# Attention's order in a piece, the joint latent norms, a last row pair by 7 products, and which row pairs of the heads and of the query latent go by 7

## The chip, the cores and the metric

The kernel runs on one core of one Trainium2 chip. The metric is the device time of one execution in microseconds, as the median of several runs; lower is better. The engines are named as in the profile: PE is TensorE's matmul, PEld its weight load, DVE VectorE, ACT ScalarE, POOL GpSimd, SP SyncE. SP issues the loads of the weights; GpSimd's queue carries the DMAs that read and write the stream x.

## The reference

A decoder trunk of two layers over 256 tokens of 2048 features in float32: retention with an MLP, then latent attention (MLA) with an MLP. What matters here:

```python
x = x + retention(rms_norm(x), w_in, w_out)      # 8 heads: q, k 256 wide, v, gate 512 wide
x = x + sq_relu_mlp(rms_norm(x), w1, w2)         # 2048 -> 8192 -> 2048, relu squared

down = rms_norm(x) @ w_kv_down                   # 512 latent columns, 64 of the rotary key
c_kv = rms_norm(down[..., :512])
k_pe = apply_rope(rms_norm(down[..., 512:]))
k_nope, v = split(c_kv @ w_kv_up)                # 16 heads of 128 and 128
c_q = rms_norm(rms_norm(x) @ w_dq)               # the query latent, 1536 wide
q_nope, q_pe = split(c_q @ w_uq)                 # each normed per head, q_pe rotated
p = softmax(causal(scale * (q_nope @ k_nope.T + q_pe @ k_pe.T)))
x = x + (p @ v) @ w_o
x = x + sq_relu_mlp(rms_norm(x), w1, w2)
```

## The kernel before

**Products in three matmuls.** Each float32 operand is split into a rounded part `h` and a rest `l` (`split`, lines 187 to 198): ScalarE casts the first (L191), VectorE subtracts it (L192). A product is then three matmuls, high x high, high x low and low x high (L362 to L364 in `gemm_pair`, L252 to L254 in `piece`). The weights come from HBM in tiles `raw` (four buffers) by SP's queue; their parts `wh` and `wl` have five buffers each. A name with an ending such as `rp_wl` is the group's name and the tile's: `rp` is a head's values and gate, `rq` and `rk` its queries and keys, `ro` the output of retention, `u` and `d` an MLP's up- and down-projection, `kd` the latent's down-projection, `dq` the query latent, `ku` the keys and values from the latent, `uq` the queries, `wo` attention's output, `x_mlp` and `xh` the stream x in SBUF and in HBM.

**Row pairs by 7 or by 8 products.** `quad` (L288) takes one weight tile of two by two blocks (a row pair by a column pair) and the two halves of the tokens: by 8 plain products, in two splits of 1024 columns, or by 7 (L315 on). The latter needs sums of the activations (`more`, made ahead by `with_sums`) and sums of the weight blocks, made in the tile by VectorE (L327, L330 and L331); it has four splits, of 1024, 512, 1024 and 1024 columns. An 8-product row pair is 24 matmuls of 128x512, a 7-product one 21. `gemm_pair` (L339) runs the row pairs of one column pair; its `kinds` says which go by 7. The tables on line 50 hold them: `FOUR`, `THREE`, `HEAD` for a head's values and gate and half of the output of retention, `QUERY` for the query latent. A column pair has eight row pairs, and mostly nine PSUM tiles are wanted over it: `acc` (four banks), `tp` (two) for `p1` and `p5`, `at` (a double bank) for `p6` and `p7`. At the end `pair_out` copies six accumulators by ScalarE (L379) and makes four sums on VectorE.

**What sets the order.** All engines work in the order in which the program writes their instructions. Work that has to come later is put in a queue with a number of ticks (`later`, L99); a tick follows every weight tile, and what is due is then written, by due time and then in the order of entry. `need` writes what is queued until an operand exists.

**The latent.** `downed` (L874) gets the down-projection. Per token half it makes two reciprocal roots (`rstd`, L166: two operations on GpSimd each), and VectorE scales and rotates the key. Two ticks later the latent is transposed in two steps of four (`turn_latent`; tiles `ckvtp`), three ticks later the key (`turn`; `kpe_tp`); both kinds use the two `tp` banks.

**Attention's pieces.** For each of eight pairs of heads, `query` reads the accumulator twice for each token half (L1010 and L1012). Three tiles of `uq` later its `turn` transposes the query's plain part (`qntp`, read by L1042) and its rotary part (`qptp`, cast to `qpe` by L1047). Three tiles after that `score` makes the scores and the softmax; three (later two) after that its `turn` transposes the probabilities (`ptp`, two banks of three transposes, each copied to `pt` by L1097), and `values` follows. Thus the steps of three neighbouring pairs fall on one tick, each in the order in which it was entered. All these transposes use the two `tp` banks.

**The last down-projection.** In the second MLP the last group of four hidden blocks is taken for columns 0 to 1023 by `gemm_pair`, and for columns 1024 to 1535 and 1536 to 2047 by `gemm` from a weight array of its own (`mlp_w2t`), 32 products of three matmuls each. The stream x was loaded into SBUF for all four blocks (`x_tiles`, L139), is added to (L477) and each block goes out by a DMA (`finish`). In the other groups `to_home` (L151) adds results to the copy of x in HBM (`x_home`) by accumulating DMAs of GpSimd's queue.

Of the kernel before, what the change touches and what calls it, by code (L numbers as in the profile page):

```python
# [16 lines left out]
ALU = mybir.AluOpType  # L17
# [4 lines left out]
NT = 2  # L22
# [26 lines left out]
GROUPS = (4, 4, 4, 4)  # L49
THREE, FOUR, HEAD, QUERY = (3, 5, 7), (1, 3, 5, 7), (2, 4, 6, 7), (4, 6, 7)  # L50
PI = math.pi
# [17 lines left out]
def yoco(ctx: ExitStack, tc: tile.TileContext, a):  # L69
# [28 lines left out]

    def later(n, fn):  # L99
        queue.append((clock[0] + n, next(count), fn))  # L100

    def run_first():
        i = min(range(len(queue)), key=lambda i: queue[i][:2])
        due, _, fn = queue.pop(i)
        fn()

# [31 lines left out]

    def x_tiles(name):  # L139


        def bring(b):
            both = act_tile(f"x_{name}{b}", F32)
            for t in range(NT):
                x[t][b] = both[:, t].rearrange("p i s -> p (i s)")
                nc.gpsimd.dma_start(x[t][b], x_home[t][b])

        for b in range(NB):
            later(2 * b, lambda b=b: bring(b))
# [64 lines left out]
    def stream(w, chunk, cols, name, use, done=None, before=None):  # L214
# [22 lines left out]
        if done is not None:  # L237
            queue.append((clock[0] + 1, -1, done))
        tick()
# [47 lines left out]

    def quad(w, chunk, x, mm, name):  # L288

# [12 lines left out]
        def parts(src, part):  # L302
# [35 lines left out]

    def gemm_pair(w, chunk0, act, kinds, name, done):  # L339

# [25 lines left out]
        for i in range(len(kinds)):  # L366
            need(act, i + 1)
            v, more = act[i]
            quad(w, chunk0 + i, (v, more if kinds[i] else None), mm, f"{name}{i}")
            if i == len(kinds) - 1:  # L370
                queue.append((clock[0] + 1, -1, lambda: pair_out(made, name, done)))
            tick()
# [214 lines left out]
    def first_inputs(c):  # L587

        t = f2k([2, S], f"x0t_{c}")
        nc.sync.dma_start(t, a["xt"][:, 2 * c : 2 * c + 2, :])  # L590
        v = act_tile(f"a0_{c}")
        split_act(v, t, [gain(G_MIX0 + 2 * c + j) for j in range(2)])
        act0.append(v)
        sums0.append(None)
        if c in HEAD:

            def again():
                t = f2k([2, S], f"x0s_{c}")
# [9 lines left out]
            later({2: 21, 4: 14, 6: 16, 7: 17}[c], again)  # L608

# [188 lines left out]
    def mlp(layer, act, r, done):  # L798
        w1, w2 = a[f"mlp_w1_{layer}"], a[f"mlp_w2_{layer}"]
        f0 = 0  # L800
        for gi, nf in enumerate(GROUPS):
# [3 lines left out]
            def up(c, p, hid=hid, blocks=blocks, last=last):  # L805
# [7 lines left out]
                def turn(i):  # L813
                    for q in (2 * i, 2 * i + 1):
# [7 lines left out]
                        split_act(v, u)  # L822
                        blocks.append((v, with_sums(u, name) if len(blocks) in (THREE if last else FOUR) else None))
                        hid.append(v)
# [26 lines left out]
            f0 += nf  # L851

    ss = [small(NB, f"ss2_{t}") for t in range(NT)]
# [20 lines left out]
    def downed(acc, b):  # L874
# [36 lines left out]

        later(3, turn)
        later(2, lambda: turn_latent(0))
        later(2, lambda: turn_latent(1))

# [89 lines left out]
    def query(acc, b):  # L1005
# [33 lines left out]
        def turn():  # L1039
# [7 lines left out]
            nc.scalar.copy(qpe, tp)  # L1047
            later(waits[b][1], lambda: score(b, qt, qpe))

        later(waits[b][0], turn)  # L1050

    def score(b, qt, qpe):
# [47 lines left out]

        later(waits[b][2], turn)

# [18 lines left out]

    def finish(b, acc):
        add_to_x(acc, b, None, "")
        for t in range(NT):
            queue = nc.scalar if b == NB - 1 and t else nc.sync
            queue.dma_start(a["out"][t * P : (t + 1) * P, b * 512 : (b + 1) * 512], x[t][b])

# [96 lines left out]
```

## Time and profile before

| | before |
|---|---|
| median of three runs | 2473.2 us (2472.24 to 2474.51) |
| the profiled execution | 2471.59 us |
| its span, from the first instruction to the last | 2469.8 us |
| mean granted TensorE clock | 1.000 |
| DMA | 521.05 MB, 211 GB/s over the span |

The span is on one core. Below, TensorE's busy time is given by stage: stretch, its length, and then for PE, PEld, DVE, ACT and POOL the busy time with the count of instructions, the clock, the share of DMA and GB/s.

```profile
0.00:300.00 300.00, 296.23 (x1446) 245.86 (x1447) 251.97 (x343) 186.85 (x267) 74.13 (x86) 1.00 0.64 223
...
1440.00:1600.00 160.00, 157.97 (x816) 139.83 (x815) 132.48 (x259) 108.58 (x185) 19.05 (x19) 1.00 0.51 171
1600.00:1720.00 120.00, 117.72 (x711) 109.42 (x710) 85.67 (x203) 83.81 (x182) 13.54 (x14) 1.00 0.49 167
1720.00:1830.00 110.00, 110.00 (x510) 91.45 (x509) 75.67 (x93) 64.42 (x93) 5.84 (x12) 1.00 0.58 193
```

The first stretch holds the start and the first heads, the second the latent and the query latent, the third most of attention's pieces. Where PE's busy time falls short of a stretch's length, TensorE waited: 3.8 us in the first (the loads at the start among it), 2.0 and 2.3 us in the next two, nothing in the last. Such a figure counts a matmul as busy to its modelled end, which lies after the start of the next; the time between the starts of neighbouring matmuls is the safer reading.

### The profile page before, as it was taken

Reading aid. Unit: us, or ns where it says so; the run is one execution under the profiler, and the core shown is the slowest. Engines: PE = TensorE matmul, PEld = TensorE weight load, DVE = VectorE, ACT = ScalarE, POOL = GpSimd, SP = SyncE. Lnnn points to the kernel's source line nnn. Section 1 sums busy time; section 2 is a strip of 40 time slices with the busy share of each in tenths; the row PEclk is TensorE's granted clock in tenths of the full one; section 3 lists DMA queues with packets and bytes.
Section 4 is the critical chain, followed back from the end, with each engine's and each line's share of the span. In section 5 each row is a group of like instructions: output and inputs, shape, how many; then the busy total and the mean of one; then the engine's idle time right before and its main releaser. Section 6 shows DMA issues by size and latency. Waiting matters only on the chain.

```text
span 2469.8 us, 31758 instructions
## 1 busy us (share of the span) xinstructions
PE 2456.1 (99%) x11635; PEld 2058.2 (83%) x11635; DVE 2185.4 (88%) x2838; ACT 1615.7 (65%) x2271; POOL 247.1 (10%) x310
## 2 busy tenths in 40 slices
PE   9999999999999999999999999999999999999999
PEld 7888888888888888888888888998888888888887
DVE  7799899889899999999999988776689999999996
ACT  6566656556676667667666777676566666676663
POOL 7300011000010010110110101100000101101100
PEclk9999999999999999999999999999999999999999
DMA  9655567555565685684785565545655866857854
GB/s 328 213 176 203 194 206 235 198 193 201 198 239 180 208 261 217 210 257 171 249 260 201 189 212 183 166 139 185 204 176 197 260 212 211 265 205 224 267 191 154
DMA packets 93404, 521.05 MB, mean 211 GB/s; under 512 B 11072, under 2 KB 12224, under 8 KB 40000
## 3 DMA queue, kind: packets, MB, share of 16 engines
q1 hardware_dynamic: 71712, 472.56, 54.0%
q0 software_dynamic: 21248, 46.15, 8.5%
q8 instruction: 91, 1.49, 0.2%
q14 instruction: 65, 0.53, 0.1%
q10 hardware_dynamic: 288, 0.31, 0.0%
HBM read 479.14 MB, written 39.85 MB: 210 GB/s over the span
## 4 chain that ended last, share of the span: by engine, by line
PE 92%; DVE 3%; ACT 3%; DMA 1%; issue 1%; POOL 0%; SPq 0%; ACTq 0%; POOLq 0%
PE u_c L364 7%; PE u_c L362 7%; PE u_c L363 7%; PE d_c L364 6%; PE d_c L362 6%; PE d_c L363 6%; PE rp_c L362 3%; PE rp_c L363 2%; PE rp_c L364 2%; PE rk_acc L280 2%; PE rq_acc L280 2%; PE u_p L364 2%; PE u_p L362 2%; PE u_p L363 2%; PE d_p L362 2%; PE d_p L364 2%
## 5 line engine op out<-in xcount | busy, mean ns | idle before, releaser
L191 ACT CAST u_wh<-u_raw 128x1024 fp32r<-128x1024 f32 x362 | 348.0, 992 | 207.7 <-DVE u_raw L327 100.5
L191 ACT CAST d_wh<-d_raw 128x1024 fp32r<-128x1024 f32 x358 | 344.2, 993 | 202.5 <-DVE d_raw L327 93.8
L192 DVE TENSOR_TENSOR u_wl<-u_raw,u_wh 128x1024 fp32r<-128x1024 f32 x362 | 401.8, 1142 | 47.1 <-ACT u_wh L191 41.7
L192 DVE TENSOR_TENSOR d_wl<-d_raw,d_wh 128x1024 fp32r<-128x1024 f32 x358 | 397.5, 1144 | 40.1 <-ACT d_wh L191 35.5
L362 PE MATMUL u_c<-u_wh,n 128*128 128x512 f32 x706 | 276.4, 392 | 0.0
L363 PE MATMUL u_c<-u_wl,n 128*128 128x512 f32 x706 | 275.6, 390 | 0.0
L364 PE MATMUL u_c<-u_wh,n 128*128 128x512 f32 x706 | 275.0, 390 | 0.0
L362 PE MATMUL d_c<-d_wh,hid 128*128 128x512 f32 x654 | 256.0, 391 | 0.0
L363 PE MATMUL d_c<-d_wl,hid 128*128 128x512 f32 x654 | 255.4, 390 | 0.0
L364 PE MATMUL d_c<-d_wh,hid 128*128 128x512 f32 x654 | 254.7, 390 | 0.0
L191 ACT CAST rp_wh<-rp_raw 128x1024 fp32r<-128x1024 f32 (+1 forms) x166 | 161.1, 983 | 141.1 <-DVE rp_raw L327 70.0
L192 DVE TENSOR_TENSOR rp_wl<-rp_raw,rp_wh 128x1024 fp32r<-128x1024 f32 (+1 forms) x166 | 184.9, 1136 | 25.7 <-ACT rp_wh L191 23.3
L364 PEld LDWEIGHTS u_c<-u_wh,n 128*128 128x128 f32 x706 | 132.6, 188 | 27.4
L362 PEld LDWEIGHTS u_c<-u_wh,n 128*128 128x128 f32 x706 | 132.5, 188 | 27.0
L363 PEld LDWEIGHTS u_c<-u_wl,n 128*128 128x128 f32 x706 | 132.6, 188 | 26.7
L364 PEld LDWEIGHTS d_c<-d_wh,hid 128*128 128x128 f32 x654 | 122.8, 188 | 25.5
L362 PEld LDWEIGHTS d_c<-d_wh,hid 128*128 128x128 f32 x654 | 122.8, 188 | 25.0
L363 PEld LDWEIGHTS d_c<-d_wl,hid 128*128 128x128 f32 x654 | 122.8, 188 | 24.7
L156 POOL DMA_DIRECT2D xh<-d_c x48 | 41.6, 867 | 855.9 <-ACT d_c L379 854.0
L191 ACT CAST ro_wh<-ro_raw 128x1024 fp32r<-128x1024 f32 x88 | 85.7, 997 | 59.5 <-DVE ro_raw L327 25.7
L362 PE MATMUL rp_c<-rp_wh,a 128*128 128x512 f32 x286 | 111.8, 391 | 0.0
L363 PE MATMUL rp_c<-rp_wl,a 128*128 128x512 f32 x286 | 111.4, 390 | 0.2 <-DVE rp_wl L192 0.2
(515 smaller groups left out, 6095.1 us busy)
## 6 DMA issues: line engine op xcount, KB each, us to landing
u_raw<-in_mlp_w SPq DMA_DIRECT2D x128, 1024.0 KB, 5.3
d_raw<-in_mlp_w SPq DMA_DIRECT2D x120, 1024.0 KB, 4.9
rp_raw<-in_ret_w_gv SPq DMA_DIRECT2D x56, 1024.0 KB, 5.0
ro_raw<-in_ret_w_out SPq DMA_DIRECT2D x32, 1024.0 KB, 5.0
uq_raw<-in_mla_w_uq SPq DMA_DIRECT2D x24, 768.0 KB, 4.2
rq_raw<-in_ret_w_qk SPq DMA_DIRECT2D x16, 1024.0 KB, 5.0
rk_raw<-in_ret_w_qk SPq DMA_DIRECT2D x16, 1024.0 KB, 4.8
wo_raw<-in_mla_w_o SPq DMA_DIRECT2D x16, 1024.0 KB, 4.9
```

Source lines behind the costliest of these rows:

```text
L156: nc.gpsimd.dma_start(x_home[t][2 * p + j], part, accum_op=ALU.add)
L191: nc.scalar.copy(h, src)
L192: nc.vector.tensor_tensor(l, src, h.bitcast(F32), op=ALU.subtract)
L280: nc.tensor.matmul(acc[f], wh[:, cols], a.rearrange("p i s -> p (i s)"), start=k == 0, stop=k == nk - 1)
L362: nc.tensor.matmul(dst, ah, bh, start=n == 0, stop=False)
L363: nc.tensor.matmul(dst, ah, bl, start=False, stop=False)
L364: nc.tensor.matmul(dst, al, bh, start=False, stop=n == total[key] - 1)
```

## The change

**1. Row pairs.** `HEAD` is (2, 4, 5, 7) instead of (2, 4, 6, 7), and `QUERY` (4, 5, 7) instead of (4, 6, 7). The number of products stays. The input's sums for row pair 5 are made at tick 15, where those for row pair 6 were made at 16.

**2. Order in a piece.** An entry in the queue has a rank between its due time and its number. Of what is due on one tick the probabilities' transposes now come first (-2), then the scores (-1), then all else, the query's transposes among it.

**3. Latent and rotary key.** The four reciprocal roots of both token halves come from one call of `rstds`: VectorE makes the means, GpSimd one power on 128x4. The latent is transposed one tick later instead of two, the key two instead of three.

**4. The last column pair.** Columns 1024 to 2047 go through `gemm_pair` too: row pairs 1, 3 and 5 by 7 products, the other five by 8. The last weight tile is taken by columns (`by_column` in `quad`), so that the accumulators of the fourth block end first. What the 7-product pairs leave is added to x ahead of the end (`sums_out`, after row pair 5), and `finish` adds the four accumulators and sends them out. Columns 0 to 1023 no longer come into SBUF: `first_out` adds them to x in HBM by GpSimd's DMAs and copies them from there to the output, HBM to HBM. The array `mlp_w2t` is gone.

```diff
-THREE, FOUR, HEAD, QUERY = (3, 5, 7), (1, 3, 5, 7), (2, 4, 6, 7), (4, 6, 7)
+THREE, FOUR, HEAD, QUERY = (3, 5, 7), (1, 3, 5, 7), (2, 4, 5, 7), (4, 5, 7)
...
-    def later(n, fn):
-        queue.append((clock[0] + n, next(count), fn))
+    def later(n, fn, rank=0):
+
+        queue.append((clock[0] + n, rank, next(count), fn))
...
+        if by_column:
+            b12, b22 = parts(b[:, 1:3], 0)
+            mm("c12", a(0, 0), b12)
+            mm("c12", a(0, 1), b22)
+            mm("c22", a(1, 0), b12)
+            mm("c22", a(1, 1), b22)
+            b11, b21 = parts(b[:, 0:4:3], 1)
+            mm("c11", a(0, 0), b11)
+            mm("c11", a(0, 1), b21)
+            mm("c21", a(1, 0), b11)
+            mm("c21", a(1, 1), b21)
+            return
...
+            if early and i + 1 < len(kinds) and kinds[i] and not any(kinds[i + 1 :]):
+                queue.append((clock[0] + 1, -3, 0, lambda: early(made)))
...
             if last:
-                x_tiles(f"mlp{layer}")
+                x_tiles(f"mlp{layer}", 2 * layer)
             for p in range(2):
-                if last and p and layer:
-                    for b in (2, 3):
-                        need(hid, 2 * nf)
-                        gemm(
-                            a["mlp_w2t"], (b - 2) * nf, hid, 4 * nf, 512, f"d{layer}_{gi}{b}",
-                            lambda acc, b=b: done(b, acc),
+                if last and layer:
+                    if p:
+                        gemm_pair(
+                            w2, p * 32 + 2 * f0, blocks, [i in FOUR[:3] for i in range(2 * nf)], "last", done, sums_out
+                        )
+                    else:
+                        gemm_pair(
+                            w2, 2 * f0, blocks, [i in THREE for i in range(2 * nf)], f"d{layer}_{gi}{p}", first_out
                         )
                     continue
...
+    def first_out(c):
+
+        to_home(c, 0)
+        for b in range(2):
+            for t in range(NT):
+                nc.gpsimd.dma_start(out_of(t, b), x_home[t][b])
+
+    def sums_out(c):
+
+        o = {}
+        for key in ("p1", "p5"):
+            o[key] = f2k([512], f"last_{key}")
+            nc.scalar.copy(o[key], c[key])
+        v, u = (f2k([512], f"last_{i}") for i in "vu")
+        nc.vector.tensor_tensor(v, c["p6"], o["p1"], op=ALU.add)
+        nc.vector.tensor_tensor(u, c["p7"], v, op=ALU.add)
+
+        def rest():
+            nc.vector.tensor_tensor(x[0][2], x[0][2], o["p1"], op=ALU.add)
+            nc.vector.tensor_tensor(v, o["p5"], v, op=ALU.subtract)
...
-        for t in range(NT):
-            tot = small(1, f"cktot{t}")
-            nc.vector.reduce_sum(tot, sck[t], axis=AX.X)
-            rc.append(rstd(tot, KVR, 1, f"ck{t}"))
-            spe = small(1, f"spe{t}")
-            raw = down[t][0][:, S:]
-            square_sum(raw, spe, f"kpe{t}")
-            rp = rstd(spe, ROPE, 1, f"kpe{t}")
+        tot = small(2 * NT, "cktot").rearrange("p (t i h) -> p t i h", t=NT, i=2)
+        for t in range(NT):
+            nc.vector.reduce_sum(tot[:, t, 0], sck[t], axis=AX.X)
+            square_sum(down[t][0][:, S:], tot[:, t, 1], f"kpe{t}")
+        r = rstds(tot, [KVR, ROPE], "ck")
...
-        later(3, turn)
-        later(2, lambda: turn_latent(0))
-        later(2, lambda: turn_latent(1))
+        later(1, lambda: turn_latent(0))
+        later(1, lambda: turn_latent(1))
+        later(2, turn)
...
-            later(waits[b][1], lambda: score(b, qt, qpe))
+            later(waits[b][1], lambda: score(b, qt, qpe), -1)
...
-        later(waits[b][2], turn)
+
+        later(waits[b][2], turn, -2)
...
+    def finish(c):
+        for i, (key, t, b) in enumerate((("c12", 0, 3), ("c22", 1, 3), ("c11", 0, 2), ("c21", 1, 2))):
+            nc.vector.tensor_tensor(x[t][b], c[key], x[t][b], op=ALU.add)
+            (nc.scalar if i % 2 else nc.sync).dma_start(out_of(t, b), x[t][b])
```

How the instructions stand on an engine, at three places. Line numbers of the change are higher than those of before: L1097 became L1146, L1042 L1091, L1047 L1096, L327, L330 and L331 became L339, L342 and L343.

First ScalarE in one of attention's pieces, from the fourth reading of a projection on. Before:

```order
L1012 ACTIVATE qu_14725<-uq_acc_14587,cq_r 128x384
L1042 ACTIVATE qt_14739<-qntp_14734,gqn 128x512
L191 CAST uq_wh_14901<-uq_raw 128x768
L191 CAST qt_14741<-qt_14739 128x512
L1047 CAST qpe_14750<-qptp_14745 128x512
L1097 COPY pt_14795<-ptp_14791 128x384
L1097 COPY pt_14801<-ptp_14797 128x384
L1082 ACTIVATE p_14773,den_14778<-p_14773,mx_14777 128x128 x2
L1082 ACTIVATE p_14774,den_14778<-p_14774,mx_14777 128x256 x2
```

Now:

```order
L1061 ACTIVATE qu_14711<-uq_acc_14573,cq_r 128x384
L1146 COPY pt_14724<-ptp_14720 128x384
L1146 COPY pt_14730<-ptp_14726 128x384
L191 CAST uq_wh_14887<-uq_raw 128x768
L1091 ACTIVATE qt_14776<-qntp_14771,gqn 128x512
L191 CAST qt_14778<-qt_14776 128x512
L1131 ACTIVATE p_14753,den_14758<-p_14753,mx_14757 128x128 x2
L1131 ACTIVATE p_14754,den_14758<-p_14754,mx_14757 128x256 x2
L1096 CAST qpe_14787<-qptp_14782 128x512
```

The copies of the probabilities (`pt`) went from behind the query's cast `qpe` to the place ahead of the query's first part `qt`, and `qpe` now stands behind the exponentials.

Second VectorE around row pairs 5 to 7 of the third head's values and gate (`rp25` to `rp27`). Before:

```order
L192 TENSOR_TENSOR rp25_wl1_1920<-rp25_raw_1901,rp25_wh1_1919 128x1024
L192 TENSOR_TENSOR rp26_wl0_1938<-rp26_raw_1935,rp26_wh0_1937 128x1024
L192 TENSOR_TENSOR rp26_wl1_1948<-rp26_raw_1935,rp26_wh1_1947 128x512
L327 TENSOR_TENSOR rp26_raw_1935<-rp26_raw_1935 128x1024
L330 TENSOR_TENSOR rp26_raw_1935<-rp26_raw_1935 128x512
L331 TENSOR_TENSOR rp26_raw_1935<-rp26_raw_1935 128x512
L192 TENSOR_TENSOR rp26_wl2_1958<-rp26_raw_1935,rp26_wh2_1957 128x1024
L192 TENSOR_TENSOR rp26_wl3_1968<-rp26_raw_1935,rp26_wh3_1967 128x1024
L192 TENSOR_TENSOR rp27_wl0_1980<-rp27_raw_1977,rp27_wh0_1979 128x1024
```

Now:

```order
L192 TENSOR_TENSOR rp25_wl1_1914<-rp25_raw_1901,rp25_wh1_1913 128x512
L339 TENSOR_TENSOR rp25_raw_1901<-rp25_raw_1901 128x1024
L342 TENSOR_TENSOR rp25_raw_1901<-rp25_raw_1901 128x512
L343 TENSOR_TENSOR rp25_raw_1901<-rp25_raw_1901 128x512
L192 TENSOR_TENSOR rp25_wl2_1924<-rp25_raw_1901,rp25_wh2_1923 128x1024
L192 TENSOR_TENSOR rp25_wl3_1934<-rp25_raw_1901,rp25_wh3_1933 128x1024
L192 TENSOR_TENSOR rp26_wl0_1946<-rp26_raw_1943,rp26_wh0_1945 128x1024
L192 TENSOR_TENSOR rp26_wl1_1962<-rp26_raw_1943,rp26_wh1_1961 128x1024
L192 TENSOR_TENSOR rp27_wl0_1980<-rp27_raw_1977,rp27_wh0_1979 128x1024
```

The sums of weight blocks and the four splits went from row pair 6 to row pair 5, so that a row pair by 8, with its two splits, stands between the last two by 7.

Third VectorE at the latent's turn, between the weight splits of the query latent (`dq`): the latent's low parts (`ckv`), the rotary key (`kp`, and its low part `kpp`) and sums of other activations (`n_20_sum`, `n_20_more`). Before, behind the key:

```order
L404 TENSOR_TENSOR n_20_sum<-n2u_12522,n_20_sum 128x128
L404 TENSOR_TENSOR n_30_sum<-n2u_12643,n_30_sum 128x128
L192 TENSOR_TENSOR dq_wl_13049<-dq_raw,dq_wh_13048 128x1024
L192 TENSOR_TENSOR n_20_more<-n_20_sum,n_20_more 128x2x256
L195 SCALAR_TENSOR_TENSOR ckv_12950<-ckvtp_12945,gains,ckv_12950 128x256
L195 SCALAR_TENSOR_TENSOR ckv_12960<-ckvtp_12955,gains,ckv_12960 128x256
L192 TENSOR_TENSOR n_30_more<-n_30_sum,n_30_more 128x2x256
L195 SCALAR_TENSOR_TENSOR ckv_12950<-ckvtp_12945,gains,ckv_12950 128x256
L195 SCALAR_TENSOR_TENSOR ckv_12960<-ckvtp_12955,gains,ckv_12960 128x256
```

Now:

```order
L195 SCALAR_TENSOR_TENSOR ckv_12895<-ckvtp_12890,gains,ckv_12895 128x256
L916 TENSOR_TENSOR kp_12828<-kp_12828 128x64
L195 SCALAR_TENSOR_TENSOR ckv_12905<-ckvtp_12900,gains,ckv_12905 128x256
L942 TENSOR_SCALAR kp_12839<-down_12736,ck_r 128x64
L947 TENSOR_TENSOR kpp_12834<-kp_12828,kpp_12834 128x64
L913 TENSOR_TENSOR kp_12839<-kp_12839,petab_96 128x64
L914 TENSOR_TENSOR kp_12839<-kp_12839,petab_96 128x32
L915 TENSOR_TENSOR kp_12839<-kp_12839,petab_96 128x32
L948 MEMSET kpp_12845 128x64
L916 TENSOR_TENSOR kp_12839<-kp_12839 128x64
L195 SCALAR_TENSOR_TENSOR ckv_12895<-ckvtp_12890,gains,ckv_12895 128x256
L195 SCALAR_TENSOR_TENSOR ckv_12905<-ckvtp_12900,gains,ckv_12905 128x256
```

The latent's four low parts went from behind the key and the sums to between the key's operations: two of them beside the first token half's key, two behind the second's rotation.

More of the change, by code (lines that the diff above doesn't have):

```diff
@@ L97, in yoco @@
     clock, count = [0], itertools.count()
-    def later(n, fn):
-        queue.append((clock[0] + n, next(count), fn))
+    def later(n, fn, rank=0):
+        queue.append((clock[0] + n, rank, next(count), fn))
     def run_first():
-        i = min(range(len(queue)), key=lambda i: queue[i][:2])
-        due, _, fn = queue.pop(i)
-        fn()
+        i = min(range(len(queue)), key=lambda i: queue[i][:3])
+        queue.pop(i)[3]()
     def tick():
@@ L137, in yoco, with x_tiles @@
     x = [[None] * NB for t in range(NT)]
-    def x_tiles(name):
+    def x_tiles(name, first=0):
         def bring(b):
@@ L146, in bring @@
                 nc.gpsimd.dma_start(x[t][b], x_home[t][b])
-        for b in range(NB):
+        for b in range(first, NB):
             later(2 * b, lambda b=b: bring(b))
@@ L237, in stream @@
         if done is not None:
-            queue.append((clock[0] + 1, -1, done))
+            queue.append((clock[0] + 1, -3, 0, done))
         tick()
@@ L286, in gemm_t, with quad @@
             stream(w, chunk0 + g, 2048, f"{name}{g}", use, (lambda: done(acc)) if g == n - 1 else None)
-    def quad(w, chunk, x, mm, name):
+    def quad(w, chunk, x, mm, name, by_column=False):
         raw = pool.tile([P, 2048], F32, tag="raw", bufs=4, name=f"{name}_raw")
@@ L337, in quad, with gemm_pair @@
         mm("c21", a(1, 1), u4)
-    def gemm_pair(w, chunk0, act, kinds, name, done):
+    def gemm_pair(w, chunk0, act, kinds, name, done, early=None):
         made = {}
@@ L368, in gemm_pair @@
             v, more = act[i]
-            quad(w, chunk0 + i, (v, more if kinds[i] else None), mm, f"{name}{i}")
+            by_column = early is not None and i == len(kinds) - 1
+            quad(w, chunk0 + i, (v, more if kinds[i] else None), mm, f"{name}{i}", by_column)
+            if early and i + 1 < len(kinds) and kinds[i] and not any(kinds[i + 1 :]):
+                queue.append((clock[0] + 1, -3, 0, lambda: early(made)))
             if i == len(kinds) - 1:
-                queue.append((clock[0] + 1, -1, lambda: pair_out(made, name, done)))
+                queue.append((clock[0] + 1, -3, 0, lambda: done(made) if early else pair_out(made, name, done)))
             tick()
@@ L606, in again @@
                 later(2, sum_up)
-            later({2: 21, 4: 14, 6: 16, 7: 17}[c], again)
+            later({2: 21, 4: 14, 5: 15, 7: 17}[c], again)
     ss0 = [small(NB, f"ss0_{t}") for t in range(NT)]
@@ L822, in turn @@
                         split_act(v, u)
-                        blocks.append((v, with_sums(u, name) if len(blocks) in (THREE if last else FOUR) else None))
+                        blocks.append((v, with_sums(u, name) if len(blocks) in (THREE if last and not layer else FOUR) else None))
                         hid.append(v)
@@ L851, in mlp, with out_of @@
             f0 += nf
+    def out_of(t, b):
+        return a["out"][t * P : (t + 1) * P, b * 512 : (b + 1) * 512]
+    def first_out(c):
[14 more added lines that the diff above has]
+            nc.vector.tensor_tensor(v, o["p5"], v, op=ALU.subtract)
+            nc.vector.tensor_tensor(x[1][2], x[1][2], u, op=ALU.add)
+            nc.vector.tensor_tensor(u, o["p5"], u, op=ALU.subtract)
+            nc.vector.tensor_tensor(x[0][3], x[0][3], v, op=ALU.add)
+            nc.vector.tensor_tensor(x[1][3], x[1][3], u, op=ALU.add)
+        later(1, rest)
     ss = [small(NB, f"ss2_{t}") for t in range(NT)]
@@ L883, in downed @@
         kps = []
+        tot = small(2 * NT, "cktot").rearrange("p (t i h) -> p t i h", t=NT, i=2)
         for t in range(NT):
[L885 to L891 removed]
+            nc.vector.reduce_sum(tot[:, t, 0], sck[t], axis=AX.X)
+            square_sum(down[t][0][:, S:], tot[:, t, 1], f"kpe{t}")
+        r = rstds(tot, [KVR, ROPE], "ck")
+        for t in range(NT):
+            rc.append(r[:, t, 0])
+            raw, rp = down[t][0][:, S:], r[:, t, 1]
             kp = f2k([2, 2, ROPE], f"kp{t}")
```

5 lines of the change are left out of this document (removed).

## The prediction

> **What bounds the kernel now.** I read the page's first and fourth parts, then TensorE's waits, then the timeline around each of them.
>
> ```profile
> span 2469.8 us, 31758 instructions
> PE 2456.1 (99%) x11635; PEld 2058.2 (83%) x11635; DVE 2185.4 (88%) x2838; ACT 1615.7 (65%) x2271; POOL 247.1 (10%) x310
> ...
> PE 92%; DVE 3%; ACT 3%; DMA 1%; issue 1%; POOL 0%; SPq 0%; ACTq 0%; POOLq 0%
> ```
>
> TensorE is busy for 99% of the span and is 92% of the chain that ended last. So an edit counts only if it takes matmuls away, takes a wait of TensorE away, or shortens the tail. VectorE at 88% is the runner-up: what it is late with, TensorE waits for. The waits, all of TensorE's but the three at the start (which the change leaves) and one of 0.2 us:
>
> ```profile
> engine line waited for: us in total, times, longest us
> PE ptp L1095 <- ACT qpe L1047: 2.3, 5, 0.6
> PE kpe_tp L211 <- DVE ckv L195: 1.9, 1, 1.9
> ...
> PE rq_acc L276 <- DVE rq_wl L192: 1.1, 6, 0.2
> PE ro_c L363 <- DVE ro_wl L192: 0.4, 2, 0.2
> PE rp_c L363 <- DVE rp_wl L192: 0.2, 1, 0.2
> PE dq_acc L253 <- DVE dq_wl L192: 0.2, 1, 0.2
> ```
>
> These waits are counted from the modelled end of the matmul before, which lies after the start of the next one in an unbroken run. So a wait costs more than its figure; I price each from start to start. The profiled execution took 2471.6 us with its span of 2469.8, and the median of the three runs is 2473.2. I work on the span and take the difference off the median.
>
> **Term A: nine matmuls less, 2.0 us.** The last two column blocks were 64 products of three matmuls (192); three row pairs by 7 products and five by 8 make 61 (183).
>
> ```profile
> 2449.33 0.39 PE L254 MATMUL d_acc<-d_wh,hid 128*128 128x512 f32 x1
> ...
> 2462.93 0.39 PE L254 MATMUL d_acc<-d_wh,hid 128*128 128x512 f32 x1
> ```
>
> Sixty matmuls lie between the two starts: 13.60 / 60 = 0.227 us each, though one is drawn 0.39 long. Nine are 2.04 us. The Trainium skill, "TensorE: Matmul & The Clock Gate", section on why the gap is 56 ns and not 53.3, puts a warm 512-column step at 215.7 ns; by it the term would be an estimated 1.94 us. The rows here are some 5% slower, and the measurement stands.
>
> The extra additions of a 7-product row pair are VectorE work beside TensorE's. The pattern (1, 3, 5) after a pair that ends in 7 products is the one that every other group's second pair has, and none of those shows a wait in the list; so I cost it at nothing. Without that cover, one late split costs 0.3 us.
>
> The end itself:
>
> ```profile
> 2465.14 0.24 PE d_acc L254
> 2465.38 0.02 issue
> 2465.40 0.69 DVE x_mlp L477
> ```
>
> Now as before one 128x512 addition and one output DMA stand behind the last matmul: three of the four final blocks are finished 6, 12 and 18 matmuls earlier (1.4 to 4.1 us, against 0.69 for an addition). The tail of 4.7 us (2465.14 to 2469.8) stays. The six earlier additions (some 0.6 us each) and four splits fit into the last two row pairs, 48 matmuls or 10.9 us.
>
> **Term B: the rotary key's transpose, 1.2 us.**
>
> ```profile
> 1453.53 0.63 PE L211 MATMUL kpe_tp<-cst,kpp 128*128 128x128 f32 x4 [1.85 <-DVE ckv L195]
> ```
>
> Its start is 2.24 us behind that of the matmul before (1451.29), against 0.23: 2.0 us lost. It waits for a PSUM bank that the latent's split frees. Now that split stands 24 matmuls (5.4 us) earlier and the key's transpose follows 24 matmuls later, at about 1446.1. What is late next is the key itself: its second square sum ends at 1441.0 in the trace, then come one power on GpSimd and, on VectorE, two short chains of some 0.9 us each, four halves of the latent's split at 0.4 and one sum at 0.35 (together 3.8 us).
>
> ```profile
> 1440.01 0.55 POOL L171 TENSOR_TENSOR kpe_r<-kpe_m,neg_half 128x1 f32<-128x1 f32 x1
> 1442.64 1.54 POOL L171 TENSOR_TENSOR ck_r<-ck_m,neg_half 128x1 f32<-128x1 f32 x1
> ...
> 1437.30 2.58 DVE L192 TENSOR_TENSOR dq_wl<-dq_raw,dq_wh 128x1024 fp32r<-128x1024 f32 x2 [0.78 <-ACT dq_wh L191]
> ...
> 1442.56 1.22 DVE L192 TENSOR_TENSOR dq_wl<-dq_raw,dq_wh 128x1024 fp32r<-128x1024 f32 x1
> ```
>
> The power takes 0.55 where VectorE is idle and 1.54 where it lies under a split. So the key is ready between 1445.6 and 1446.6; an interleaved cast on ScalarE (1.05) can add as much again. The new wait is 0 to 1.3 us, the gain 0.7 to 2.0; I take a wait of 0.8, gain 1.2. The Trainium skill, "SBUF — State Buffer", section "SBUF: two separate sides", says that GpSimd and VectorE take one port pair exclusively, a VectorE operation with two SBUF inputs included, and the loser waits for the whole instruction. The trace agrees (1.54 beside 1442.56). By it the one power left waits out a split as well: 1.0 us later than at 0.55, the upper end.
>
> **Term C: attention's order, 3.4 us.**
>
> ```profile
> 1639.33 0.49 PE L1095 MATMUL ptp<-cst,p 128*128 128x128 f32 x3
> 1640.20 0.55 PE L1095 MATMUL ptp<-cst,p 128*128 128x128 f32 x3 [0.38 <-ACT qpe L1047]
> 1640.51 0.42 PE L252 MATMUL uq_acc<-uq_wh,cq 128*128 128x384 f32 x1
> ...
> 1712.74 0.82 PE L1095 MATMUL ptp<-cst,p 128*128 128x128 f32 x6
> 1713.32 0.47 PE L252 MATMUL wo_acc<-wo_wh,ot 128*128 128x512 f32 x1
> ```
>
> Six transposes of probabilities take 1.18 us with the wait and 0.58 without: 0.60 lost where the list counts 0.38. So five waits of 2.3 cost 2.3 + 5 x 0.22 = 3.4 us. The second bank is held by the query's rotary part until ScalarE has cast it:
>
> ```profile
> 1637.26 0.59 ACT L1012 ACTIVATE qu<-uq_acc,cq_r 128x384 f32<-128x384 f32 x1
> 1637.72 0.70 ACT L1042 ACTIVATE qt<-qntp,gqn 128x512 f32<-128x512 f32 x1
> ...
> 1639.54 0.61 ACT L1047 CAST qpe<-qptp 128x512 fp32r<-128x512 f32 x1
> 1642.30 0.86 ACT L1097 COPY pt<-ptp 128x384 f32<-128x384 f32 x2 [2.15 <-DVE qt L192]
> ```
>
> Now the probabilities are transposed first, the scores follow (1636.97 to 1639.33, 2.3 us), then the query. The two banks must then be free of the two copies of `pt`: these stand right behind the fourth reading of the projection (done 1637.85) and take 0.86, so they end at 1638.7, while TensorE reaches the second query transpose at about 1639.5: 0.8 us to spare. Queued behind them on ScalarE are the cast of `uq`, the query's cast and the exponentials; the query's parts are read only three pieces (12 us) later. The gain lies between 0 and 3.4; I take 3.4.
>
> **Term D: other row pairs by 7, 3.4 us.** (2, 4, 6, 7) ends in two 7-product row pairs side by side, and then the accumulators are copied:
>
> ```profile
> 1479.22 0.39 PE L252 MATMUL dq_acc<-dq_wh,n 128*128 128x512 f32 x1
> 1479.78 0.50 PE L253 MATMUL dq_acc<-dq_wl,n 128*128 128x512 f32 x1 [0.18 <-DVE dq_wl L192]
> ...
> 1475.31 2.50 DVE L192 TENSOR_TENSOR dq_wl<-dq_raw,dq_wh 128x1024 fp32r<-128x1024 f32 x2
> 1478.50 3.50 DVE L192 TENSOR_TENSOR dq_wl<-dq_raw,dq_wh 128x1024 fp32r<-128x1024 f32 x3 [0.69 <-ACT dq_wh L191]
> ...
> 1475.50 1.05 ACT L191 CAST dq_wh<-dq_raw 128x1024 fp32r<-128x1024 f32 x1 [0.40 <-DVE dq_raw L331]
> 1476.46 1.06 ACT L379 COPY dq_c<-dq_c 128x512 f32<-128x512 f32 x2
> 1477.41 2.95 ACT L191 CAST dq_wh<-dq_raw 128x1024 fp32r<-128x1024 f32 x3
> ```
>
> The start comes 0.56 us after the last one, so 0.34 is lost: two copies (0.95) hold the cast back, VectorE idles 0.69 and its split is 0.34 late. The list has ten such waits (6 + 2 + 1 + 1): 3.4 us. With (2, 4, 5, 7) the neighbours 4 and 5 lie in the middle, where no copies follow. The same chain then has its cast 0.95 earlier and VectorE no gap, so the split is 0.69 earlier: 0.69 - 0.34 = 0.35 us to spare. A row pair by 8 takes TensorE 5.44 us and VectorE two splits (2.5), so it refills the stock before the last one by 7 and the copies. The bounds are 0 (all ten waits move to row pair 6) and 3.4; I take 3.4, as the cause of each is in the rows. The number of matmuls does not change here.
>
> **Sum.** 2.0 + 1.2 + 3.4 + 3.4 = 10.0 us: a span of 2459.8, a profiled run of 2461.6, a median of **2463.2**.
>
> **Rivals.** *D only moves* (2466.6): the spare 0.35 us is thin, and any small operation on VectorE between row pairs 4 and 6 eats it. For it: 0.2 us of wait already tips ten places. Against it: the instructions listed there are the same chain without copies. *C only changes hands* (2466.6): the query's transposes wait for the copies of `pt` instead. It decides if the copies come over 0.8 us later than worked out.
>
> *The output copies end last* (slower). Two column blocks now leave over GpSimd's queue: eight accumulating DMAs into the copy of x in HBM, a wait for their landing, then four copies from HBM to HBM, which this trace never shows.
>
> ```profile
> 2304.52 1.56 POOL L156 DMA_DIRECT2D xh<-d_p  x1
> 2305.06 3.22 POOL L146 DMA_DIRECT2D x_mlp<-xh  x4
> ...
> xh<-d_p POOLq DMA_DIRECT2D x24, 256.0 KB, 10.1
> ...
> x_mlp<-xh POOLq DMA_DIRECT2D x16, 256.0 KB, 8.9
> ```
>
> That pair's matmuls ended near 2294, so the last sum is issued 11 us later and lands after 10: 21 us. Here the pair's matmuls end near 2413.8 (2421.8 less B, C, D), so the copies go out at about 2435 to 2438; at the 8.9 us of a load from there they land at 2447, 13 us ahead of the end. It decides when one takes over 22 us; to be slower than 2469.8 it must take over 32. The price is each microsecond beyond, say 2476 at 38 us.
>
> **Chances.** Forecast 0.62; D moves 0.15; C changes hands 0.12; both, or small new waits elsewhere, to 2470: 0.08; output copies last 0.03. Nothing at all in the terms (the products not saved) has no chance worth a number: the instruction list has nine matmuls less. A measurement of this kernel tells about 0.2% (4.9 us) from no change, so under 2468.3 is faster: forecast and both single rivals, less a little, 0.86. Within 0.2%: 0.11. Slower: 0.03. The range takes in both single rivals and B's and D's bounds: 2460.8 (B without a wait and 1.6 us of the small waits that the list does not name gone too) to 2468.
>
> **What would show it.** A right: no `d_acc`, 183 matmuls of `last` 0.227 apart, the tail again 4.7 us. B: `kpe_tp` in the waits with under 1.3 us. C: no wait of `ptp`, `qntp` or `qptp` in the list. D: no wait of `rq_acc`, `ro_c`, `rp_c`, `dq_acc` for a split; moved, if `rp_c` and `ro_c` wait about ten times in row pair 6. The forecast is wrong if the list keeps over 3 us of waits behind the first 20 us, or if GpSimd's last DMA lands last.

## The result and the profile after

| | before | the change |
|---|---|---|
| median beside each other | 2472.93 us (6 runs) | 2459.57 us (6 runs, 2458.6 to 2461.6) |
| a second time, `e_change_again` | 2472.5 us (9 runs) | 2460.41 us (5 runs) |
| profiled execution, span | 2471.59 us, 2469.8 us | 2459.91 us, 2458.1 us |

The ratio is 0.9946 with a 95% interval from 0.9935 to 0.9957, the second time 0.9949 (0.9936 to 0.9963). Over all runs, the change has a median of 2460.2 us (11 runs) and before 2472.7 (45 runs): 12.5 us less. The change is faster, and by more than was forecast: 2463.2 was expected, and 2459.57 lies 1.2 us under the range. One execution of `e_order`, the profiled one, took 3505.57 us at a granted clock of 0.656; it is left out of that run's median, and the trace is read from `e_order_again`.

The first and the fourth part of the page of the change:

```profile
span 2458.1 us, 31782 instructions
PE 2448.9 (100%) x11626; PEld 2057.3 (84%) x11626; DVE 2199.1 (89%) x2859; ACT 1617.8 (66%) x2280; POOL 251.1 (10%) x311
...
PE 99%; ACT 1%; DVE 0%; DMA 0%; issue 0%; POOL 0%; SPq 0%; ACTq 0%; POOLq 0%
```

TensorE's share of the chain that ended last went from 92 to 99%. All its waits in the change (line, what ended it; total us, times, longest):

```profile
PE rg_acc L252 <- ACT a L194: 1.9, 2, 1.3
PE idle L133 <- DVE zeros L130: 1.2, 1, 1.2
PE rq_acc L276 <- DVE rq_wl L192: 1.1, 1, 1.1
PE ao L1156 <- ACT qt L1091: 0.6, 1, 0.6
```

The first three lie in the first 34 us. Behind the start one wait is left, `ao`, and it is new. To see where the time went, I take the first matmul of each stage from TensorE's timeline (start, length). Before:

```profile
81.48 1.57 PE L665 MATMUL sc<-rq_q,rk_q 128*128 128x256 f32 x8
...
725.59 0.39 PE L362 MATMUL u_c<-u_wh,n 128*128 128x512 f32 x1
...
1405.15 0.30 PE L252 MATMUL kd_acc<-kd_wh,n 128*128 128x320 f32 x1
...
1544.52 0.42 PE L252 MATMUL uq_acc<-uq_wh,cq 128*128 128x384 f32 x1
...
1682.75 0.39 PE L252 MATMUL wo_acc<-wo_wh,ot 128*128 128x512 f32 x1
...
2421.68 0.39 PE L252 MATMUL d_acc<-d_wh,hid 128*128 128x512 f32 x1
...
2464.97 0.39 PE L254 MATMUL d_acc<-d_wh,hid 128*128 128x512 f32 x1
```

And in the change:

```profile
82.33 0.92 PE L682 MATMUL sc<-rq_q,rk_q 128*128 128x256 f32 x3
...
721.55 0.39 PE L376 MATMUL u_c<-u_wh,n 128*128 128x512 f32 x1
...
1401.09 0.30 PE L252 MATMUL kd_acc<-kd_wh,n 128*128 128x320 f32 x1
...
1537.68 0.42 PE L252 MATMUL uq_acc<-uq_wh,cq 128*128 128x384 f32 x1
...
1672.62 0.39 PE L252 MATMUL wo_acc<-wo_wh,ot 128*128 128x512 f32 x1
...
2412.41 0.39 PE L376 MATMUL last_c<-last_wh,hid 128*128 128x512 f32 x1
...
2453.68 0.39 PE L378 MATMUL last_c<-last_wh,hid 128*128 128x512 f32 x1
```

The differences of neighbouring rows give the ledger; the last line is the span less the last matmul's start, to a tenth, as the span is given:

| stage | before | change | gain | forecast |
|---|---|---|---|---|
| start, to the first score of retention | 81.48 | 82.33 | -0.85 | 0 |
| heads and output of retention (part 1) | 644.11 | 639.22 | 4.89 | 3.06 |
| first MLP | 679.56 | 679.54 | 0.02 | 0 |
| latent and query latent (parts 3 and 1) | 139.37 | 136.59 | 2.78 | 1.54 |
| queries, attention (part 2) | 138.23 | 134.94 | 3.29 | 3.4 |
| output of attention, second MLP | 738.93 | 739.79 | -0.86 | 0 |
| last two column blocks (part 4) | 43.29 | 41.27 | 2.02 | 2.0 |
| tail | 4.8 | 4.4 | 0.4 | 0 |

From the first score of retention to the end that is 12.5 us, which is what the medians over all runs show. Nine of the forecast's ten waits of part 1 lie in the second line (9 x 0.34), the tenth in the fourth (1.2 + 0.34).

### The profile page after: what moved, and what is told of

Read it like the earlier page. It is cut to its first block, busy times and chain, and to the rows that moved or that the text cites. A ratio compares the mean times of both kernels' runs of the same rounds, so it can differ in the third digit from the quotient of the medians.

```text
span 2458.1 us, 31782 instructions
## 1 busy us (share of the span) xinstructions
PE 2448.9 (100%) x11626; PEld 2057.3 (84%) x11626; DVE 2199.1 (89%) x2859; ACT 1617.8 (66%) x2280; POOL 251.1 (10%) x311
## 4 chain that ended last, share of the span: by engine, by line
PE 99%; ACT 1%; DVE 0%; DMA 0%; issue 0%; POOL 0%; SPq 0%; ACTq 0%; POOLq 0%
PE u_c L378 7%; PE u_c L376 7%; PE u_c L377 7%; PE d_c L377 7%; PE d_c L378 7%; PE d_c L376 7%; PE rp_c L377 3%; PE rp_c L378 3%; PE rp_c L376 3%; PE rk_acc L280 2%; PE rq_acc L280 2%; PE u_p L376 2%; PE u_p L378 2%; PE u_p L377 2%; PE d_p L376 2%; PE d_p L377 2%
## 5 line engine op out<-in xcount | busy, mean ns | idle before, releaser
L191 ACT CAST d_wh<-d_raw 128x1024 fp32r<-128x1024 f32 x342 | 327.4, 989 | 185.5 <-DVE d_raw L339 93.9
L192 DVE TENSOR_TENSOR d_wl<-d_raw,d_wh 128x1024 fp32r<-128x1024 f32 x342 | 378.2, 1140 | 30.8 <-ACT d_wh L191 26.2
```

The lines of the kernel that those rows point to most:

```text
L191: nc.scalar.copy(h, src)
L192: nc.vector.tensor_tensor(l, src, h.bitcast(F32), op=ALU.subtract)
```

## The experiments

Each is before with a part of the change, unless said otherwise. "Behind the start" means from the first score of retention to the last matmul: 2383.49 us before, 2371.35 with the change. "From start to start" counts how much later a matmul starts behind its neighbour than in an unbroken run.

**Each part alone.** First the last column pair (the whole of the diff's part 4, no other part).

> Before with the last column pair of the change alone (part 4). Theory 1, the parts are independent stalls and matmuls: nine matmuls less at 0.227 us are 2.0 us, and a tail that is 0.4 us shorter in the trace of the change; the profiled span is 2.4 us under that of before, all waits of TensorE stay. Theory 2, the gain beyond the forecast hides in the end of the kernel (other queues, no load of two column blocks of x): over 3.5 us.

Measured: 2470.03 us against 2472.77 (11 and 29 runs; ratio 0.9991, 0.9982 to 1.0), 2.38 us less behind the start and a tail of 4.5; behind the start the waits are those of before. From the first to the last matmul of the two blocks, 41.26 us, as in the change. Theory 1: 2.0 us of matmuls and a part of the tail. The rest is scatter of the earlier stages, in which retention's stretch differs by up to 0.6 us between profiles of the same code: 644.11 us in before, 643.55 here and 643.69 to 643.88 in five others. So each part's gain behind the start holds some 0.2 to 0.6 us of this scatter.

The joint norms with the earlier turns:

```diff
+        r = rstds(tot, [KVR, ROPE], "ck")
...
-        later(3, turn)
-        later(2, lambda: turn_latent(0))
-        later(2, lambda: turn_latent(1))
+        later(1, lambda: turn_latent(0))
+        later(1, lambda: turn_latent(1))
+        later(2, turn)
```

> Before with the joint norms and the earlier turns of latent and rotary key alone (part 3). Theory 1: the wait of the rotary key's transpose goes whole, 2.0 us from start to start (the forecast had a rest of 0.8 us, gain 1.2), as in the trace of the change. Theory 2: the wait is gone in the change only because earlier parts moved the neighbouring splits; then a rest of 0.5 us or more is left here and the gain is 1.5 us or less.

Measured: 2471.65 us against 2472.77 (ratio 0.9994, 0.9985 to 1.0003), 1.53 us less behind the start. No wait of the key is left in the list, but its first transpose starts 0.25 us late (0.48 behind the last matmul, where 0.227 is a step) and a later one of the four 0.29:

```profile
1448.08 0.39 PE L364 MATMUL dq_c<-dq_wh,n 128*128 128x512 f32 x1
1448.56 0.95 PE L211 MATMUL kpe_tp<-cst,kpp 128*128 128x128 f32 x4
```

That is a rest of 0.54: theory 2, by a little.

The ranks, `score` -1 and the probabilities' `turn` -2:

> Before with the ranks in attention's pieces alone (part 2). Theory 1: the five waits of the probabilities' transposes go (3.1 us from start to start), and one new wait of about 0.9 us comes before the last but two values (ao), as in the trace of the change: 2.2 us less. Theory 2: the new wait comes from the other parts: no wait of ao, 3.1 us less. Theory 3 (the forecast): 3.4 us less.

> The ranks alone again, for a profile at full clock (the median of e_order is 1.9 us under before). Theory 1: the five waits of the probabilities' transposes are gone, and the wait of about 0.9 us before the fifth pair's values (ao) is there without the other parts. Theory 2: no such wait; then it belongs to another part.

Measured: 2470.70 us (ten runs) against 2472.77 (ratio 0.999, 0.9981 to 0.9999); `e_order_again`, one run, 2469.59 us against 2472.62, 2.79 less behind the start. Its waits have no `ptp`, and instead:

```profile
PE ao L1105 <- ACT qt L1041: 0.6, 1, 0.6
```

From start to start that is 0.74 us, and 0.10 at the matmul behind it. The new wait belongs to the ranks themselves: theory 1.

The row pairs, `HEAD` (2, 4, 5, 7) and `QUERY` (4, 5, 7), with the input's sums at tick 15:

> Before with the row pairs 4 and 5 in place of 4 and 6 or 6 alone (part 1). Theory 1: each of the ten waits costs 0.34 us at its start and 0.105 us at the start of the next matmul but one step; ten make 4.4 us, and two single waits of 0.4 and 0.3 us go with them: 4.4 to 5.1 us less. Theory 2 (the forecast): 0.34 each, 3.4 us less. Theory 3: the waits move to row pair 5 or 6: under 1.5 us less.

Measured: 2465.54 us against 2472.77 (ratio 0.9972, 0.9961 to 0.9984), 6.70 us less behind the start. All ten waits are gone, and so are two others of the same stretch: that of `o` for `vl` (0.34 and 0.11 at its next) and one of 0.18 and 0.11 at `rp_p`; one of 0.10 and 0.11 has come at another `rp_p`. And the rotary key's wait, which this part wasn't meant to touch, is 1.01 instead of 2.01 us from start to start. None of the three theories had this last piece. The four parts alone add up to 13.4 us behind the start, more than the 12.14 of all together: a part of the key's wait is counted both here and with the joint norms, and the scatter of before is counted four times.

**Whose is the key's wait?** Only `QUERY`:

> Only the query latent's row pairs 4, 5 and 7 in place of 4, 6 and 7. Theory 1: this part alone makes the rotary key's wait 1.0 us shorter (2.0 to 1.0, as with all row pairs), since it moves the query latent's splits beside the latent, and takes the one wait of dq_acc (0.45 us): 1.4 us less on the span before the start phase is counted; the nine waits of the heads and of retention's output stay. Theory 2: the key's wait is shorter because of the heads' row pairs (all later work starts at another phase): it stays at 2.0 us here.

Measured, one run of each: 2470.28 us against 2472.62, 1.93 us less behind the start. The wait of the query latent is gone, those of the heads stand, and:

```profile
PE kpe_tp L211 <- DVE ckv L195: 0.9, 1, 0.9
```

Theory 1: the key's wait is 1.01 us from start to start. The stage of the latents is 1.82 us shorter: 1.00 at the key, 0.45 at the query latent, and 0.37 in four matmuls of the latent's own projection that each started some 0.1 us late in before. The second half of the rotary key is first touched on VectorE at 1444.26 us, 38.63 behind the first `kd` matmul (1405.63); in before it was 39.97 (1445.12 less 1405.15). So the whole chain of latent and key runs 1.3 us earlier when row pair 5's block is scaled for its sums rather than row pair 6's. That ScalarE's two scalings of the later block stood in front of the square sums in before is a reading of the timeline; no run isolates it.

The turns without the joint norms:

> Before with the earlier turns of latent and rotary key alone, and the eight single norm operations on GpSimd kept. Theory 1 (the key itself is late next, so the turns are worth nothing without the joint power): the key's last part ends near 1448.4 us as before, 2.3 us or more behind the place of its transpose, so the wait of kpe_tp is 2 to 3 us and the gain none. Theory 2 (the banks alone were the hold-up): a wait of 0.6 us or less, 1.4 us or more gained.

```profile
PE kpe_tp L211 <- DVE kpp L898: 0.4, 1, 0.4
```

Measured: 0.61 us of wait from start to start, 1.19 us less behind the start and 1.33 in the stage; 2472.39 us in one run. That is much nearer to theory 2 (0.6 or less, 1.4 or more gained) than to theory 1. The row names the releaser: no longer the latent's part `ckv`, but the key's own low part `kpp`. So the earlier turns did most of it, and the joint norms add 0.1 to 0.3 us. The last 0.5 goes in the change, where `QUERY` has the key ready 1.3 us earlier; that it is `QUERY` and no other part was not run beside the joint norms. In the change the key's low part ends at 1441.66, when its transpose is due:

```profile
1441.44 0.22 DVE L947 TENSOR_TENSOR kpp<-kp,kpp 128x64 fp32r<-128x64 f32 x1
...
1441.67 0.60 PE L211 MATMUL kpe_tp<-cst,kpp 128*128 128x128 f32 x4
```

It has nothing to spare.

**What covers the probabilities' copies?** The ranks without that of the scores (0 instead of -1):

> The ranks without that of the scores: the probabilities' transposes come first, and five of the sixteen score matmuls instead of all stand between them and the query's. Theory 1 (the forecast's mechanism: the scores cover the copies of the probabilities, 0.8 us to spare of 2.3): some 1.6 us of cover are missing, so the query's transposes wait 0.5 to 1 us in each of five pieces, and the kernel is 2 to 3 us slower than with both ranks. Theory 2 (putting the probabilities first is enough): no wait of qntp or qptp, the same time as with both ranks.

```profile
PE qntp L210 <- ACT pt L1096: 3.2, 5, 0.8
...
PE ao L1105 <- ACT qt L1041: 0.8, 1, 0.8
```

2473.74 us against 2472.62, one run each, and 4.1 above `e_order_again`. Theory 1, and more than its 2 to 3 us: the wait changes hands when the scores don't all stand between the probabilities' and the query's transposes.

**Are the copies at a column pair's end the cause of the ten waits?** They are made twice:

```diff
             nc.scalar.copy(o[key], c[key])
+            if key in ("c22", "c12") and name[:2] in ("rp", "ro", "dq"):
+                nc.scalar.copy(o[key], c[key])
```

> Before with the copies of c22 and c12 made twice at the end of each column pair of the heads, of retention's output and of the query latent (two copies of 0.48 us more on ScalarE, same values). Theory 1 (the forecast's: the copies behind two neighbouring row pairs by 7 hold back the next cast): the ten waits grow from 0.34 us to between 0.8 and 1.3 us, 5 to 9.5 us more in all. Theory 2 (VectorE's stock alone decides, ScalarE has room): the waits stay near 0.34 us, under 1 us more in all.

```profile
PE rq_acc L276 <- DVE rq_wl L192: 2.8, 7, 0.5
...
PE o L687 <- DVE vl L195: 0.8, 1, 0.8
PE o L686 <- ACT vh L194: 0.8, 1, 0.8
...
PE ro_c L363 <- DVE ro_wl L192: 0.3, 2, 0.2
PE rp_c L363 <- DVE rp_wl L192: 0.2, 1, 0.2
```

2476.53 us against 2472.62, one run each, and 3.09 us more behind the start. Neither theory's size. In front of `rq` and `dq` the start of the waiting matmul came 0.54 to 0.69 us late instead of 0.34; in front of `ro` and `rp` it stayed; the first head's values lost 1.6 us more. The timeline shows why. First, a 7-product row pair adds nothing to `c22`, so its copy and the doubled one stand some 7 us earlier (136.29 and 136.89 us), ahead of other casts. Only one copy more stands in front of the cast that is late, the third here:

```profile
143.92 1.06 ACT L379 COPY rp_c<-rp_c 128x512 f32<-128x512 f32 x2
144.87 0.60 ACT L381 COPY rp_c<-rp_c 128x512 f32<-128x512 f32 x1
145.35 2.01 ACT L191 CAST rq_wh<-rq_raw 128x1024 fp32r<-128x1024 f32 x2
```

VectorE's gap behind it grew from 0.69 to 1.17, by this one copy, in front of `rq`, `ro` and `dq` alike. Second, the built program does not keep strictly to the order in which the code writes the instructions: here TensorE has matmuls with the high part, which need no split, ahead of the one that waits, one more than in before at `rq` and `dq` and two more at `ro` and `rp`:

```profile
353.48 0.84 PE L362 MATMUL ro_c<-ro_wh,y 128*128 128x512 f32 x3
354.49 0.50 PE L363 MATMUL ro_c<-ro_wl,y 128*128 128x512 f32 x1 [0.17 <-DVE ro_wl L192]
```

So the split is 0.48 later everywhere, and the wait is 0.34 + 0.48 less 0.227 for each of these matmuls: an estimated 0.59 and 0.37, where 0.54 to 0.69 and 0.33 to 0.34 were measured. The mechanism is that of theory 1, with half the copies and a stream that takes up a part.

The same on the change:

> The change with the copies of c22 and c12 made twice, as in e_copies_before. Theory 1 (the copies now come behind a row pair whose splits have 1.4 us to spare, so ScalarE has room for them): no wait of rq_acc, ro_c, rp_c or dq_acc for a split; what is left of e_copies_before's loss is that of the first head's values (o), up to 1.9 us. Theory 2 (ScalarE's copies cost wherever they stand): five waits of 0.2 us or more at rq_acc.

```profile
PE rq_acc L276 <- DVE rq_wl L192: 0.2, 1, 0.2
```

One wait of 0.40 us at 157 us, and 0.59 us more than the change behind the start. No wait in front of any other group. Theory 1: with the neighbouring row pairs by 7 away from the end, ScalarE has room there for the copies.

**Can the new wait go?** The change with the fifth pair's values one tick earlier (`(3, 3, 3, 1)` in `waits`), and the change itself beside it:

> The change with the values of the fifth pair of heads one tick earlier, ahead of the last query's transposes. Theory 1 (ao waits because the bank of the query's transposes is read late, behind three casts of wo on ScalarE): the wait of 0.8 to 0.9 us goes, the span behind the start is 0.9 us shorter than with the change. Theory 2 (the wait then moves to the last query's transposes, qntp or qptp): no gain.

> The change itself again, beside before on one chip, for a second draw of its start. Theory 1 (the stages behind the start are fixed, the start phase varies from run to run by some 2 us, and the profiled execution of before had a lucky one): from the first score of retention to the last matmul the same 2371.3 us as in the first profile within 0.2, with a start between 81.5 and 84.2; the median 12.5 to 13.5 us under before. Theory 2 (the change makes the start itself slower, by the earlier second load of an input): the start is again at 82.3 or later and never near 81.5.

```profile
1679.61 0.66 PE L211 MATMUL qptp<-cst,qpp 128*128 128x128 f32 x4 [0.67 <-DVE ot L192]
```

With the earlier values `ao` no longer waits, and the last query's rotary part waits 0.83 us for the bank that `ao` now holds. 2371.35 us behind the start, the same as the change; medians 2460.23 and 2460.41. Theory 2: the wait moves on with the bank. `e_change_again` takes 2371.56 us behind the start, and its start is 83.20; `e_values_early`, the same code up to there, has 81.26. So the 0.85 us that the start lost in the first profile is not the change's.

No run was measurably faster than the change.

## Why the prediction was wrong

The forecast named the right four places and the right sign of each, and its sum was 10.0 where 12.5 were gained.

- **Term D was mis-sized, and is the step that failed: 3.4 forecast, 6.7 alone (6.4 without the scatter of before).** The mechanism held: the waits went and did not move, and the copies lie behind them. But "0.34 is lost" counted only the waiting start, and the sum took ten times that for the most that D could gain. The matmul behind it is late as well, by 0.105 us each time: 0.34 behind the waiting one, where 0.227 is a step. In before:

```profile
1479.78 0.50 PE L253 MATMUL dq_acc<-dq_wl,n 128*128 128x512 f32 x1 [0.18 <-DVE dq_wl L192]
1480.12 0.40 PE L254 MATMUL dq_acc<-dq_wh,n 128*128 128x512 f32 x1
1480.36 0.39 PE L252 MATMUL dq_acc<-dq_wh,n 128*128 128x512 f32 x1
```

  Ten times, that is 1.05 us. Two waits beside the ten, 0.45 and 0.29 us, went with the same edit; the working left the first out and did not see the second. And 1.0 us of the key's wait and 0.4 us in the latent's projection hung on `QUERY`, where the working gave the key to B alone.
- **Term B was right in its mechanism: once the banks come free, "what is late next is the key itself".** The runs show a rest of 0.61 (turns alone) and 0.54 (with the joint norms), where 0.8 was taken. That the rest is zero in the change was not foreseen; with `QUERY` the key is ready 1.3 us earlier. The one power that is left took 1.93 us there, beside a split of VectorE, where the working's upper end had 1.54, and the key was still ready when its transpose was due. The stage gained 2.78, where B and D's one wait had 1.54.
- **Term C was 1.0 too high.** The five waits went, and their stage gained 3.29: their starts were 0.71, three times 0.54, and 0.76 late, 3.1 us where 3.4 were counted from the list. The cover of the scores was the right reason (`e_probs_first`). Not seen was `ao`: the last query's transposes wait for ScalarE behind three casts of `wo`, and TensorE, no longer held up just before, reaches the values earlier. In the change:

```profile
1677.09 2.94 ACT L191 CAST wo_wh<-wo_raw 128x1024 fp32r<-128x1024 f32 x3
1679.93 0.69 ACT L1091 ACTIVATE qt<-qntp,gqn 128x512 f32<-128x512 f32 x1
...
1680.67 0.70 PE L1156 MATMUL ao<-pt,v 128*128 128x256 f32 x2 [0.64 <-ACT qt L1091]
```

  The stage that holds it lost 0.86 us. The rival "C only changes hands" looked at the wrong transposes.
- **Term A was right: 2.02 us for nine matmuls, 0.227 apart.** The tail was taken as unchanged and is 0.4 shorter. Up to the issue of the last DMA it is as before (1.1 us behind the last matmul's start); the difference lies behind the issue. Of the DMA share in a window of 10 us (before) and 9 us (change) around the end, 40 slices each:

```profile
DMA  0000000000000000000000000899998000000000
```

```profile
DMA  0000000999100899200899200899200000000000
```

  Before, the last two blocks leave together, 0.68 us apart; now the four leave 1.36 us apart, and the last has the DMA engines to itself. That this is the 0.4 us fits the rows; no run isolates it.
- **The rival with the output copies did not happen.** GpSimd issues its last copy 18.4 us ahead of the end, at 2439.71 us where 2435 to 2438 was worked out, and the copies land in 5.7 us (median), where 8.9 was taken from the loads in before (6.3 in the change):

```profile
2439.71 0.52 POOL L880 DMA_DIRECT2D out<-xh  x1 [4.30 <-DMA xh<-d_p]
```

- **The range was too narrow because its lower end rested on the same sizes.** It let B go to its bound and 1.6 us of small waits go too, but no term could exceed its price in the list. Of the 3.6 us between 2463.2 and 2459.57, 2.5 are the terms, 0.5 is the base (2473.2 from three runs, 2472.7 from 45), and 0.6 that the change's first six runs lie under its 11.

## What to carry to other kernels

Price a wait of a pipelined engine from the rows around it, start to start, up to where the steps are regular again: the list of waits gave 0.2, the waiting start 0.34, the whole place 0.45. Where an edit moves work on the engines that feed a wait, that wait is not another term's alone; take each edit's effect on every wait of its stretch. And when a stall is taken away on an engine that shares two buffers among several users, follow those two buffers to the end of the stage: some of the gain comes back at the next user.

## What the runs showed of the hardware

The start differs from run to run by up to 3 us. The first score of retention, in kernels that have the same code up to there, starts at 81.48, 81.59, 82.10, 82.12, 82.28, 83.33, 83.49 and 83.84 us, and with the new row pairs at 81.26, 82.30, 82.33, 83.20 and 84.33. One part is TensorE's clock. The window of 12 to 16 us, first in before and then in `e_norms`; after the five engines' busy times stands the granted clock:

```profile
12.00:16.00 4.00, 4.00 (x19) 3.32 (x18) 4.00 (x9) 3.14 (x7) 0.00 (x0) 1.00 1.03 370
```

```profile
12.00:16.00 4.00, 4.00 (x13) 3.09 (x12) 4.00 (x9) 3.06 (x6) 0.02 (x1) 0.59 1.04 379
```

There 13 matmuls are counted where 19 were, the slow ones 0.427 us apart; it follows a wait of 1.8 us for the first input, which before has with 1.5. But `e_retime` waited 2.4 us there and kept its clock. The Trainium skill, "TensorE: Matmul & The Clock Gate", part 1 on the clock gate, says that the window over which the engine's activity is judged runs freely, so that the same kernel has another number of slow matmuls in each run. The traces agree that the number differs: behind 12 us `e_norms` has eight slow steps and before none, in the same code. That the window runs freely, no run here shows.

Another part is the start's tables on GpSimd beside VectorE's splits. In the change's chain that ended last, one split of 128x1024, 1.22 us elsewhere, is

```profile
31.47 2.29 DVE rq_wl L192
```

and TensorE's `rq_acc` waits 1.1 us behind it. GpSimd's operation had started first there (31.38 to 32.67). In `e_values_early`, with the same code, the split started first (31.47, for 1.22 us) and GpSimd's operation, at 31.53, took 2.32 us instead of 1.29; `rq_acc` starts 0.24 us late. In these two traces the one that comes second is the one that takes longer, by 1.0 to 1.1 us. So a start that one profile shows is a draw, and stages are compared from behind it.
